# Two PSUM banks for the first pair's keys and queries, and one rotary product from GpSimd to VectorE

## The chip, the cores and the metric

One core of a Trainium2 chip runs the whole kernel. The metric is the device time of one execution in microseconds (us), as the median of several runs. The engines are named as the profile names them: PE is TensorE (PEld its weight loads), DVE is VectorE, ACT is ScalarE, POOL is GpSimd and SP is SyncE, which here only issues DMAs. Each engine works through its own instructions in a fixed order and waits on semaphores for the others.

## What is computed

One encoder layer on 512 tokens of width 1024, in float32: layer norm, one input projection, latent attention with 8 heads beside a convolution branch, an output projection with a residual norm, and a mixture of 16 experts. The part around the change, cut from the reference:

```python
h = layer_norm(x, emb_ln_g, emb_ln_b)
proj = jnp.einsum('bsd,df->bsf', h, w_in[l])
# attention: proj[..., :c1] gives queries, proj[..., c1:c2] keys and values, proj[..., c2:c3] the rotary key
q = jnp.einsum('bsr,rf->bsf', rms_norm(cq, q_norm_g), w_qb).reshape(B, S, H, QK_NOPE_DIM + QK_ROPE_DIM)
kv = jnp.einsum('bsr,rf->bsf', rms_norm(ckv, kv_norm_g), w_kvb).reshape(B, S, H, QK_NOPE_DIM + V_HEAD_DIM)
q = jnp.concatenate([q[..., :QK_NOPE_DIM], rope(q[..., QK_NOPE_DIM:], positions)], axis=-1)
k_pe = jnp.broadcast_to(rope(kr[:, :, None, :], positions), (B, S, H, QK_ROPE_DIM))
k = jnp.concatenate([kv[..., :QK_NOPE_DIM], k_pe], axis=-1)
# softmax(q k^T) v, in blocks of 128 queries
# convolution branch: a * sigmoid(g), depthwise conv of width 31, layer norm, silu
mix = jnp.einsum('bsf,fd->bsd', jnp.concatenate([attn_out, conv_out], axis=-1), w_o[l])
h = layer_norm(DEEPNORM_ALPHA * h + mix, ln1_g[l], ln1_b[l])
h = layer_norm(DEEPNORM_ALPHA * h + expert_choice_moe(h, ...), ln2_g[l], ln2_b[l])
```

`rope` multiplies the rotary part by cosines and adds the part with swapped halves multiplied by sines.

## The kernel before

The work falls into two stages. The first ends near 273.6 us with the routing of tokens to experts. The second runs the 16 experts in turn (L1205 for gate and up, L1291 for down), 2048 KB of weights per DMA, through a ring of tiles that were used by the first stage (`stream`, L128; its DMAs are issued at L135, L145 and L161).

In the first stage nearly every product is made of three matmuls (`mm3`, L260 to L264): operands are split into a high part, copied by ScalarE, and a low part, a subtraction on another engine (`split`, L230 to L232). A projection of the input (`project`, L404) is 24 matmuls into one PSUM bank. A bank is one tile of 128x512 float32, and there are eight: three named `pj`, two `tr`, and one each of `st`, `cn` and `cv` (`bank`, L270).

Around the change the program reads, in this order. `rotary(0)` and `rotary(1)` (L604) make the rotary parts of the queries of four heads each, in bank `cn`: 9 matmuls, then `rope` (L515): ScalarE copies the bank to `raw` (L517), VectorE shuffles it (L519), POOL multiplies `raw` by the cosines (L520), VectorE multiplies the shuffled copy by the sines (L521) and adds the two (L522), and the result is split. `rope` is also used once before, for the rotary key. `glu(3, 4)` (L434) makes the last of four convolution groups: two projections in two `pj` banks, a tanh on ScalarE that reads the second (L439), a product on VectorE that reads the first (L440), four taps on ScalarE and POOL (L448, L449, L451) and 27 on VectorE (L457), marked as filler, which is taken when nothing else is due. Then come copies of the rotary key into the key tiles (L629 on POOL, L631 on ScalarE), `keys(0)` with 6 matmuls and `queries(0)` with 9 (`heads`, L638), each in one bank that two high parts on ScalarE and two low parts on VectorE empty, the V tiles (L659: four times 6 matmuls, each in a `pj` bank, copied out at L663), and the attention itself: `scores` (L737, two `pj` banks a step), `transpose_p` (L754, bank `tr`), `p_v` (L770). Keys and queries of the later pairs use bank `cn`, with the attention running. Behind it stand the first half of the output projection (`output(0, ...)`, L860, with L872), the convolution's norm (L801, L814), whose result feeds the second half, and the routing.

The order of instructions on each engine isn't that of the text. A planner takes the instruction with the earliest place in the program among those it holds ready by a simulated clock, gives out banks in the same pass, and only the stretches marked as ordered keep a written order. The order on the chip is then fixed.

Of the kernel before, what the change touches and what calls it, by code (L numbers as in the profile page):

```python
# [12 lines left out]
OP = mybir.AluOpType  # L13
# [33 lines left out]
def layer_kernel(ctx, tc, x, positions, emb_ln_g, emb_ln_b, w_in, q_norm_g, w_qb, kv_norm_g, w_kvb,  # L47
                 conv_w, conv_b, conv_ln_g, conv_ln_b, w_o, ln1_g, ln1_b, w_router,
                 w_gate, w_up, w_down, ln2_g, ln2_b, rope_rows, out):
    nc = tc.nc  # L50
# [34 lines left out]
    def quarters(t):  # L85
        return [t[:, j * 512:(j + 1) * 512] for j in range(4)]
# [23 lines left out]
    def quarter_tile(q, dt=F32):  # L110
        return slots.tile([128, S], dt, name=f"q{q}")

    def pair_tile(dt=F32R):
        return slots.tile([128, 2, S], dt, name="sq", bufs=2)
# [115 lines left out]
    def split(hi, lo, src, eng):  # L230
        scalar(nc.scalar.activation(hi, src, AF.Identity))  # L231
        pin(eng, eng.tensor_tensor(lo, src, hi.bitcast(F32), op=OP.subtract))  # L232
# [27 lines left out]
    def mm3(p, a, b, start, stop, **kw):  # L260

        tensor(nc.tensor.matmul(p, a[0], b[0], start=start, stop=False, **kw))  # L262
        tensor(nc.tensor.matmul(p, a[0], b[1], start=False, stop=False, **kw))  # L263
        tensor(nc.tensor.matmul(p, a[1], b[0], start=False, stop=stop, **kw))  # L264

    with ExitStack() as pre:
# [3 lines left out]
        def bank(kind="pj"):  # L270
            return ps.tile([128, 512], F32, name=kind, bufs={"pj": 3, "tr": 2, "st": 1, "cn": 1, "cv": 1}[kind])
# [3 lines left out]
        def tmp():  # L275
            n_tmp[0] += 1
            return quarter_tile(n_tmp[0] % 4)
# [34 lines left out]
        def split_win(g):  # L312

            name, c0, n = WIN_GROUPS[g]
            raw = raws.pop(g)
            hi, lo = (slot(i, F32R).rearrange("p (c n) -> p c n", c=8) for i in win_slots[g % 4])
            for j in range(2):
                win[c0 + 128 * j] = (hi, lo, 128 * j)
                for a in range(2):
                    cs, ns = slice(4 * a, 4 * a + 4), slice(128 * j, 128 * j + 128)  # L320
                    if name == "q2" and j:
                        for c in range(4 * a, 4 * a + 4):
                            kb = raw[:, c, None, 128:160].to_broadcast([128, 4, ROPE])
                            h4, l4 = (z[:, c, 128:].rearrange("p (r n) -> p r n", r=4) for z in (hi, lo))
                            nc.scalar.activation(h4, kb, AF.Identity)
                            pin(nc.gpsimd, nc.gpsimd.tensor_tensor(l4, kb, h4.bitcast(F32), op=OP.subtract))
                    else:
                        split(hi[:, cs, ns], lo[:, cs, ns], raw[:, cs, ns], nc.gpsimd)
                    yield
# [28 lines left out]
        def run(*gens):  # L358
            for g in gens:
                for _ in g:  # L360
                    pass
# [31 lines left out]
        for c in range(DC):  # L393
            p = bank("tr")
# [9 lines left out]
        def project(c0, kind="pj"):  # L404
            p = bank(kind)
            hi, lo, j = win[c0]
            for c in range(DC):
                mm3(p, (hi[:, c, j:j + 128], lo[:, c, j:j + 128]), hT[c], c == 0, c == DC - 1)
            return p
# [24 lines left out]
        def glu(j, n_act=0):  # L434

            pa = project(QR + KVR + ROPE + j * 128)
            pg = project(QR + KVR + ROPE + CC + j * 128)
            sg = tmp()
            nc.scalar.activation(sg, pg, AF.Tanh, scale=0.5)  # L439
            nc.vector.scalar_tensor_tensor(hp[j][:, CW // 2:CW // 2 + S], sg, 1.0, pa, op0=OP.add, op1=OP.mult)  # L440
            src = [hp[j][:, k:k + S] for k in range(CW)]
            w = [cw[:, j, k:k + 1] for k in range(CW)]

            part = bank("cv")
            for k in range(n_act):
                if k:
                    pt = tmp()
                    nc.scalar.activation(pt, src[k], AF.Identity, scale=w[k])  # L448
                    nc.gpsimd.tensor_tensor(cva[j], cva[j], pt, op=OP.add)  # L449
                else:  # L450
                    nc.scalar.activation(cva[j], src[k], AF.Identity, scale=w[k], bias=vc("cb", j))  # L451
            with filler():
                for k in range(n_act, CW):
                    if k == 0:
                        nc.vector.tensor_scalar(part, src[k], w[k], vc("cb", j), op0=OP.mult, op1=OP.add)
                    else:
                        nc.vector.scalar_tensor_tensor(part if k < CW - 1 else cva[j], src[k], w[k],  # L457
                                                       cva[j] if k == n_act else part, op0=OP.mult, op1=OP.add)


        sinS, cosT = lat[2:]
# [50 lines left out]

        shuf = [(i + 16) % 32 for i in range(32)]

        def rope(p, dst):  # L515
            raw = tmp()
            nc.scalar.activation(raw, p, AF.Identity)  # L517
            sh = tmp()
            nc.vector.stream_shuffle(sh, raw, shuf)  # L519
            nc.gpsimd.tensor_tensor(raw, raw, cosT, op=OP.mult)  # L520
            nc.vector.tensor_tensor(sh, sh, sinS, op=OP.mult)  # L521
            nc.vector.tensor_tensor(sh, raw, sh, op=OP.add)  # L522
            split(dst[0], dst[1], sh, nc.gpsimd)
# [20 lines left out]
        for j in range(2):  # L544
            p = project(QR + j * 128)
# [4 lines left out]
        pk = project(QR + KVR)  # L550
        add_up(pst, sq)
        kpe = (quarters(s17)[3], quarter_tile(4, F32R))
        rope(pk, kpe)
        run(split_win(5))

        wq_raw = []
# [9 lines left out]
        for j in range(3):  # L566
            p = project(j * 128)
# [33 lines left out]
                split(hi, lo, wkvb[:, c, :].rearrange("p (h f) -> p h f", h=HEADS)[:, :, o:o + 64], nc.gpsimd)  # L601
        qr = {}

        def rotary(g):  # L604
            p = bank("cn")
            for c in range(3):
                w = tuple(wqr[c][:, k * 256 + g * 128:k * 256 + (g + 1) * 128] for k in range(2))
                mm3(p, w, cqn[c], c == 0, c == 2)
            qr[g] = pair_tile()
            rope(p, (qr[g][:, 0], qr[g][:, 1]))  # L610

        rotary(0)
        rotary(1)
        glu(3, 4)


# [28 lines left out]
        def keys(i, kind="cn"):  # L645
            qe, ke, qo, ko = qk[i % 2]
            heads(i, wkn, 2, ckvn, ke, ko, kind)

        def queries(i, kind="cn"):
            qe, ke, qo, ko = qk[i % 2]  # L650
            heads(i, wqn, 3, cqn, qe, qo, kind)
            for n, dst in ((2 * (i % 2), [z[64:96] for z in qe]), (2 * (i % 2) + 1, [z[32:64] for z in qo])):
                for k in range(2):
                    copy_to(k, dst[k], qr[i // 2][32 * n:32 * n + 32, k, :].bitcast(F32), 32 * n)

        keys(0, "pj")
        queries(0, "pj")
        vt = quarters(slot(14))
        for i in range(4):  # L659
            p = bank()  # L660
# [45 lines left out]
        for a in range(2):  # L706
            nc.vector.tensor_tensor(wr2[:, :, a], wr2[:, :, 1], gb[:, a * DC:(a + 1) * DC, None].to_broadcast([128, DC, E]),
                                    op=OP.mult)
# [452 lines left out]
    for e in range(E):  # L1161
# [19 lines left out]
        for k, j in order:  # L1181
            p = pgu[k]
# [76 lines left out]
        for b in range(2):  # L1259
            p = ps.tile([128, 512], F32, name="sg", bufs=2) if b else ps.tile([128, 512], F32, name="tr")  # L1260
# [19 lines left out]
        for c in range(8):  # L1280
# [4 lines left out]
            for a in range(2):  # L1285
                f = 2 * c + a
                b, g, j = f // 8, (f // 4) % 2, f % 4
# [66 lines left out]
```

## Time and profile before

| | us |
|---|---|
| median of 3 runs | 1196.94 (1196.2 to 1197.55) |
| profiled execution | 1194.84 |
| its span, first to last instruction | 1192.4 |
| PE busy | 1119.9 |
| DVE busy | 383.5 |
| ACT busy | 249.6 |
| POOL busy | 200.4 |
| start of the first expert's gather | 273.6 |

Times in the views are counted from the start of the span. Busy time of PE is modelled, since its matmuls are pipelined: back to back they follow one another faster than each one's shown duration. In a timeline a row gives start, duration, engine, line, operation, output and inputs by name, the count of merged instructions, and in brackets the idle time ahead of it and what ended that.

### The profile page before, as it was taken

The numbers are of one execution on the slowest core, as the hardware profiler recorded it, in microseconds if no ns is written. First come the engines' busy times: TensorE is split into PE (matmuls) and PEld (weight loads), VectorE is DVE, ScalarE is ACT, GpSimd is POOL, SyncE is SP. The second block draws the span as 40 slices with busy tenths as digits, with TensorE's granted clock in tenths as the row PEclk, the third lists the DMA queues.
The fourth block names the chain that finished last, engine by engine and source line by source line (L and its number), as shares of the span: only waits on it lengthen the run. The fifth ranks groups of instructions, "written<-read, shape, count | busy, mean of one in ns | idle before, by whom it ended". The sixth has DMA issues, their size and how long they took to land.

```text
span 1192.4 us, 13664 instructions
## 1 busy us (share of the span) xinstructions
PE 1119.9 (94%) x5573; PEld 526.4 (44%) x5573; DVE 383.5 (32%) x901; ACT 249.6 (21%) x461; POOL 200.4 (17%) x234
## 2 busy tenths in 40 slices
PE   5898998999999999999999999989998999899996
PEld 3687775785434343433433343324332423243422
DVE  6899998452110311131012102110311031102241
ACT  4545687321101110100110011001110101012110
POOL 6768577210000600000000000000000000000040
PEclk9999999999999999999999999999999999999999
DMA  6421024777999999999999999999999999999997
GB/s 201 138 73 45 10 72 159 271 272 293 378 426 428 428 428 425 428 429 429 426 426 428 426 427 429 428 426 428 427 428 427 428 429 426 427 428 429 427 426 304
DMA packets 43825, 422.85 MB, mean 355 GB/s; under 512 B 5194, under 2 KB 13203, under 8 KB 18034
## 3 DMA queue, kind: packets, MB, share of 16 engines
q1 hardware_dynamic: 41600, 419.18, 84.8%
q10 hardware_dynamic: 2082, 2.53, 0.6%
q8 instruction: 43, 0.70, 0.2%
q0 software_dynamic: 80, 0.26, 0.1%
q14 instruction: 20, 0.16, 0.0%
HBM read 419.60 MB, written 2.36 MB: 354 GB/s over the span
## 4 chain that ended last, share of the span: by engine, by line
PE 56%; DMA 31%; DVE 9%; ACT 2%; issue 1%; POOL 1%; ACTq 0%; POOLq 0%; SPq 0%; DVEq 0%
PE gu L1205 24%; DMA b<-in_w_up_dram 16%; PE py L1291 13%; DMA b<-in_w_down_dram 9%; PE sg L1048 4%; DVE cv L457 4%; DMA b<-in_w_gate_dram 3%; PE sg L1095 3%; PE pj L262 2%; PE pj L263 2%; PE pj L264 2%; PE st L776 1%; DMA s<-in_w_in_dram 1%; PE tr L1070 1%; ACT s L231 1%
## 5 line engine op out<-in xcount | busy, mean ns | idle before, releaser
L1205 PE MATMUL gu<-b,xg 128*64 128x512 f32 x1920 | 447.1, 600 | 29.2 <-DMA b<-in_w_up_dram 20.2
L1205 PEld LDWEIGHTS gu<-b,xg 128*64 128x64 f32 x1920 | 124.5, 136 | 268.9 <-issue 206.0
L1291 PE MATMUL py<-b,sq 128*64 128x512 f32 x976 | 227.3, 601 | 1.1 <-DMA b<-in_w_down_dram 1.0
L1060 POOL COPY sq<-oh 128x256 f32<-128x256 f32 x16 | 5.9, 400 | 747.1 <-PE sg L1262 747.1
L1291 PEld LDWEIGHTS py<-b,sq 128*64 128x64 f32 x976 | 62.8, 136 | 104.7 <-issue 91.2
L1085 DVE SCALAR_TENSOR_TENSOR q<-py,gates,q 64x512 fp32r<-64x512 f32 x30 | 22.5, 749 | 235.5 <-ACT q L1084 235.5
L262 PE MATMUL pj<-s,s 128*128 128x512 f32 x189 | 76.5, 413 | 9.8 <-ACT q L439 5.3
L1048 PEld LDWEIGHTS sg<-oh,h 128*128 128x128 f32 x512 | 65.3, 197 | 45.5 <-issue 43.8
L1048 PE MATMUL sg<-oh,h 128*128 128x128 f32 x512 | 76.5, 293 | 1.3 <-DVE oh L1039 0.7
L1222 DVE TENSOR_TENSOR sq<-sq,gu 128x512 f32<-128x512 f32 x30 | 20.6, 687 | 175.2 <-PE gu L1205 175.2
L263 PE MATMUL pj<-s,s 128*128 128x512 f32 x189 | 75.7, 401 | 0.0
L1098 DVE TENSOR_TENSOR b<-sg,b 128x512 f32<-128x512 f32 x64 | 43.9, 690 | 85.9 <-PE sg L1095 81.7
L232 POOL TENSOR_TENSOR s<-s,s 128x512 fp32r<-128x512 f32 (+2 forms) x54 | 65.6, 1239 | 16.0 <-ACT s L231 11.0
L1266 ACT ACTIVATE sq<-tr 128x512 f32<-128x512 f32 x16 | 9.6, 597 | 275.6 <-PE tr L1262 275.6
L1049 ACT ACTIVATE xg<-sg,gbp 128x128 f32<-128x128 f32 x64 | 29.2, 457 | 163.0 <-PE sg L1048 163.0
L457 DVE SCALAR_TENSOR_TENSOR cv<-s,q,cv 128x512 f32<-128x512 f32 x83 | 62.2, 750 | 1.7
L264 PE MATMUL pj<-s,s 128*128 128x512 f32 x157 | 61.9, 397 | 0.0
L1227 ACT ACTIVATE sq<-gu 128x512 f32<-128x512 f32 x32 | 18.9, 597 | 189.6 <-PE gu L1205 189.5
L244 DVE SCALAR_TENSOR_TENSOR mask<-tr,aff,ones_b 128x128 bf16<-128x128 f32 x84 | 26.1, 348 | 100.6 <-PE tr L242 100.6
L1095 PE MATMUL sg<-q,q 128*128 128x512 f32 (+1 forms) x128 | 44.9, 448 | 0.3 <-DVE b L1098 0.3
L262 PEld LDWEIGHTS pj<-s,s 128*128 128x128 f32 x189 | 36.4, 194 | 19.3 <-ACT q L439 6.3
L1084 ACT ACTIVATE q<-py,gates 64x512 fp32r<-64x512 f32 x30 | 20.5, 682 | 93.0 <-PE py L1291 72.7
(287 smaller groups left out, 1095.1 us busy)
## 6 DMA issues: line engine op xcount, KB each, us to landing
b<-in_w_gate_dram SPq DMA_DIRECT2D x60, 2048.0 KB, 33.6
b<-in_w_up_dram SPq DMA_DIRECT2D x60, 2048.0 KB, 31.8
b<-in_w_down_dram SPq DMA_DIRECT2D x59, 2048.0 KB, 33.8
s<-in_w_gate_dram SPq DMA_DIRECT2D x8, 1024.0 KB, 6.5
s<-in_w_in_dram SPq DMA_DIRECT2D x12, 512.0 KB, 5.3
s<-in_w_up_dram SPq DMA_DIRECT2D x6, 1024.0 KB, 7.0
s<-in_w_down_dram SPq DMA_DIRECT2D x6, 1024.0 KB, 10.3
s<-in_w_o_dram SPq DMA_DIRECT2D x4, 1024.0 KB, 7.4
```

What stands on the lines that cost most here:

```text
L232: pin(eng, eng.tensor_tensor(lo, src, hi.bitcast(F32), op=OP.subtract))
L244: vector(nc.vector.scalar_tensor_tensor(mask[:, u], here, aff[:, u, e:e + 1], ones_b if u < t else before, op0=OP.is_le, op1=OP.mult, accu ...
L262: tensor(nc.tensor.matmul(p, a[0], b[0], start=start, stop=False, **kw))
L263: tensor(nc.tensor.matmul(p, a[0], b[1], start=False, stop=False, **kw))
L264: tensor(nc.tensor.matmul(p, a[1], b[0], start=False, stop=stop, **kw))
L457: nc.vector.scalar_tensor_tensor(part if k < CW - 1 else cva[j], src[k], w[k], cva[j] if k == n_act else part, op0=OP.mult, op1=OP.add)
L1048: tensor(nc.tensor.matmul(here, rows, oh[:, t, :], start=t == 0, stop=t == TT - 1))
L1049: nc.scalar.activation(xg[:, cc, :], here, AF.Identity, scale=gbp[:, 0, cc:cc + 1], bias=gbp[:, 1, cc:cc + 1])
L1095: tensor(nc.tensor.matmul(pp[h], g[h][rs, ts], parts[h][k][rs, :], start=k == 0, stop=k == 1))
L1098: nc.vector.tensor_tensor(a, pp[h], a, op=OP.add)
L1205: tensor(nc.tensor.matmul(p[b][g * 64:(g + 1) * 64, :], xg[:, c, s * CAP:(s + 1) * CAP], ws[a][2 * b + g], start=c == 0, stop=c == DC - 1))
L1291: tensor(nc.tensor.matmul(py[x * 64:(x + 1) * 64, :], hT2[:, b, j, g * 64:(g + 1) * 64], w[2 * a + hf], start=f == 0 and not last, stop=f ...
```

## The change

`rope` and `rotary` take the engine for the product by the cosines as an argument. The rotary key and the first set of queries pass POOL, as before; the second set passes VectorE. `keys(0)` and `queries(0)` take banks named `tr` where they took `pj`.

```diff
-        def rope(p, dst):
+        def rope(p, dst, eng):
             raw = tmp()
             nc.scalar.activation(raw, p, AF.Identity)
             sh = tmp()
             nc.vector.stream_shuffle(sh, raw, shuf)
-            nc.gpsimd.tensor_tensor(raw, raw, cosT, op=OP.mult)
+            eng.tensor_tensor(raw, raw, cosT, op=OP.mult)
             nc.vector.tensor_tensor(sh, sh, sinS, op=OP.mult)
             nc.vector.tensor_tensor(sh, raw, sh, op=OP.add)
             split(dst[0], dst[1], sh, nc.gpsimd)
...
-        rope(pk, kpe)
+        rope(pk, kpe, nc.gpsimd)
...
-        def rotary(g):
+        def rotary(g, eng):
...
-            rope(p, (qr[g][:, 0], qr[g][:, 1]))
-
-        rotary(0)
-        rotary(1)
+            rope(p, (qr[g][:, 0], qr[g][:, 1]), eng)
+
+        rotary(0, nc.gpsimd)
+
+        rotary(1, nc.vector)
         glu(3, 4)
...
-        keys(0, "pj")
-        queries(0, "pj")
+
+        keys(0, "tr")
+        queries(0, "tr")
```

## Rows read from the trace of the kernel before

**Rows 1.** The page: busy us of each engine, share of the span, instructions.
```profile
PE 1119.9 (94%) x5573; PEld 526.4 (44%) x5573; DVE 383.5 (32%) x901; ACT 249.6 (21%) x461; POOL 200.4 (17%) x234
```

**Rows 2.** Busy time by stretch, in the header's order, with granted clock and DMA.
```profile
core 0: us, PE busy (x) PEld busy (x) DVE busy (x) ACT busy (x) POOL busy (x), PEclk, DMA share, GB/s
100.00:112.40 12.40, 12.40 (x56) 10.06 (x54) 12.19 (x20) 7.47 (x13) 11.71 (x11) 1.00 0.00 0
112.40:128.00 15.60, 9.98 (x38) 7.74 (x38) 15.32 (x23) 10.77 (x19) 14.44 (x12) 0.89 0.11 35
128.00:180.00 52.00, 51.53 (x320) 38.80 (x320) 49.03 (x84) 39.85 (x86) 30.27 (x45) 1.00 0.12 42
180.00:215.00 35.00, 30.97 (x193) 20.75 (x189) 28.49 (x48) 24.77 (x53) 22.54 (x24) 1.00 0.54 183
...
273.60:500.00 226.40, 224.61 (x1137) 92.06 (x1137) 34.62 (x120) 28.53 (x52) 21.34 (x20) 1.00 0.96 403
500.00:1192.00 692.00, 653.14 (x3161) 245.32 (x3157) 131.33 (x377) 71.86 (x126) 19.03 (x25) 1.00 1.00 422
```

**Rows 3.** Timeline of PE, 112 to 128 us: start, duration, instruction, idle before.
```profile
112.16 0.39 PE L264 MATMUL pj<-s,s 128*128 128x512 f32 x1
...
116.08 0.79 PE L262 MATMUL pj<-s,s 128*128 128x512 f32 x1 [3.35 <-ACT q L439]
...
120.82 0.39 PE L264 MATMUL pj<-s,s 128*128 128x512 f32 x1
...
123.81 0.47 PE L262 MATMUL pj<-s,s 128*128 128x512 f32 x1 [2.27 <-DVE s L232]
...
127.99 0.40 PE L262 MATMUL pj<-s 96*128 96x512 f32 x1
```

**Rows 4.** Timeline of ACT, 115 to 123 us.
```profile
115.46 0.57 ACT L439 ACTIVATE q<-pj 128x512 f32<-128x512 f32 x1
...
117.91 0.81 ACT L451 ACTIVATE s<-hp,q 128x512 f32<-128x512 f32 x1 [1.41 <-DVE hp L440]
...
122.30 0.63 ACT L231 ACTIVATE sq<-q 128x512 fp32r<-128x512 f32 x1 [1.73 <-DVE q L522]
```

**Rows 5.** Timeline of DVE, 110 to 123 us.
```profile
110.49 0.73 DVE L519 STREAM_SHUFFLE q<-q 128x512 f32<-128x512 f32 x1
...
111.76 0.82 DVE L521 TENSOR_TENSOR q<-q,s 128x512 f32<-128x512 f32 x1
...
117.20 0.67 DVE L440 SCALAR_TENSOR_TENSOR hp<-q,pj 128x512 f32<-128x512 f32 x1
...
119.06 3.21 DVE L522 TENSOR_TENSOR q<-q,q 128x512 f32<-128x512 f32 x1
...
122.97 0.69 DVE L232 TENSOR_TENSOR s<-pj,s 64x512 fp32r<-64x512 f32 x1
```

**Rows 6.** Timeline of POOL, 112 to 122 us.
```profile
112.10 5.03 POOL L629 TENSOR_TENSOR s<-sq,zero 32x512 fp32r<-32x512 f32 x4
117.20 1.29 POOL L520 TENSOR_TENSOR q<-q,s 128x512 f32<-128x512 f32 x1
118.45 2.03 POOL L629 TENSOR_TENSOR s<-q,zero 64x512 fp32r<-64x512 f32 x2
120.44 1.27 POOL L730 TENSOR_TENSOR h<-h,s 128x512 f32<-128x512 f32 x1
```

**Rows 7.** Line 522 over the span: duration in ns, lowest, median and highest.
```profile
L522 DVE TENSOR_TENSOR q<-q,q x3: 676/687/3215, 74.3 to 119.1; 128x512 f32<-128x512 f32 x3
```

**Rows 8.** Timeline of POOL and DVE, 224 to 233 us.
```profile
224.78 2.67 POOL L232 TENSOR_TENSOR sq<-s,s 128x512 fp32r<-128x512 f32 x2 [0.33 <-ACT s L231]
...
232.42 0.69 DVE L872 SCALAR_TENSOR_TENSOR h<-h,pj 128x512 f32<-128x512 f32 x1 [2.03 <-PE pj L264]
```

**Rows 9.** Groups of instructions, 60 to 215 us: busy us, mean ns, idle before.
```profile
L457 DVE SCALAR_TENSOR_TENSOR cv<-s,q,cv 128x512 f32<-128x512 f32 x76 | 57.0, 750 | 1.6
```

**Rows 10.** What the DMA queue of SP waited for, 60 to 330 us.
```profile
SPq L161 <- PE gu L1205: 25.9, 6, 6.1
```

## The prediction

> **What bounds the kernel now.** I read four views, from coarse to fine. The engine totals come first [rows 1]: TensorE is busy for 94% of the span and nothing else comes near, but that is a mean over stages with different limits. The table by stretches [rows 2] separates them. From 500 us on the DMA engines are full (share 1.00, 422 GB/s) and TensorE does 653 us of work in 692: the experts run at the pace of their weights. From 273.6 to 500 TensorE (224.6 of 226.4) and the DMA (0.96) are both full. So the expert stage has a fixed length, counted from its start: its ring of weight tiles refills only as experts' matmuls free tiles [rows 10], and a microsecond won or lost ahead of 273.6 moves the end by about one microsecond. The change lies ahead of it, so the question is what ends last between 100 and 273.6.
>
> There [rows 2] TensorE is full from 100 to 112.4, has 51.5 us of work in the 52 from 128 to 180, and 31.0 in the 35 from 180 to 215. The one large hole is from 112.4 to 128: 9.98 us of 15.6, at a granted clock of 0.89, so part of it at 1.2 instead of 2.4 GHz. VectorE is nearly full all the while (12.2 of 12.4, 15.3 of 15.6, 49.0 of 52). A large part of that, 57.0 us between 60 and 215 in its largest group alone, is the depthwise convolution (L457), which fills every gap [rows 9]. So I look for what TensorE waits for in the hole, and for what VectorE may still carry.
>
> **The hole, step by step.** TensorE issues its last matmul of the fourth GLU projection at 112.16, apart from one tiny transpose does nothing until 116.08, and is released by ScalarE's tanh (L439) [rows 3]. The 15 matmuls that follow, to 120.82, are 9 of queries(0) and 6 of the first V tile, so keys(0) is already done and queries(0) waits for a `pj` bank: there are three, the projection's two halves hold two and keys(0) the third. The tanh comes at 115.46 with no idle time ahead of it on ScalarE [rows 4]: it stands behind a run of copies. The 15 matmuls then take 4.96 us (116.08 to 121.04, one step after the last one's start); at the pace of the full stretch before, 56 instructions in 12.4 us or 0.22 us each [rows 2], they take 3.3. The second wait, 2.27 us to 123.81, is a V tile waiting for a bank that VectorE's low part (L232, 122.97) frees [rows 3, 5]. That one is late because VectorE stands in L522, the last step of the second rotary set, from 119.06 for 3.21 us. The first score matmul comes at 127.99 [rows 3].
>
> **Part 1, the banks.** keys(0) and queries(0) take the two `tr` banks. Their earlier user, the transposes of the input, is long over, and their next user, the transposes of the probabilities, needs the splits of keys and queries through the scores anyway; this adds no wait. queries(0) then needs no bank of the projection's and follows at 112.4; the first V tile goes to the `pj` bank that keys(0) used to hold. Those 15 matmuls end at 112.4 + 3.3 = 115.7, against 121.04: 5.3 us earlier, of which about 3.7 is the wait and 1.6 the slower matmuls after it. The next V tile takes the bank that the tanh leaves at 116.0 (115.46 + 0.57 [rows 4]), the third the one that L440 leaves at 117.9 [rows 5], the fourth that of the first once it is copied out.
>
> What is late next is ScalarE and VectorE, not TensorE. If only matmuls counted, the scores would start at 112.4 + 33 × 0.22 (queries, four V tiles) + 0.6 for the small transposes = 120.3, which is 7.7 us earlier: one end. The other end is no gain at all, the scores at 128.0: the splits (L231, L232) need ScalarE and VectorE, whose order is fixed in advance and holds the copies ahead of the tanh. In between I count ScalarE: in the hole it idles 15.6 - 10.77 = 4.8 us [rows 2], all of it behind the tanh, of which 1.41 is a wait for L440 and 1.73 a wait for L522 [rows 4], and the rest waits for V tiles and low parts. Without idle time its work from 115.46 to 128.0 is 12.5 - 4.8 = 7.7 us and ends at 123.2; keeping the wait for L440, which VectorE's order sets and the change doesn't touch, 124.6. Some 0.6 of that work (one V tile) needn't come ahead of the scores, which gives about **124.0, a gain of 4.0 us**. I take this because it is nearest to rows that stay.
>
> **Part 2, the product by the cosines.** For the second set, POOL loses one L520 of 1.29 us (at 117.20) [rows 6] and VectorE gains one 128x512 product. POOL's op ran 6 us after its input was shuffled (110.49 [rows 5]), behind 5.03 us of copies [rows 6]; on VectorE it can follow the shuffle at once. No other engine's wait is added: VectorE now waits for ScalarE's copy only, which it did for the shuffle. The first set's product and the key's stay on POOL. The trace shows no such product on VectorE, but L521 and L522 are the same form: L522 took 676, 687 and 3215 ns [rows 7]. So the cost is 0.68 to 3.2 us; I take 0.7. Against it L522 no longer stands at 119.06, and if it then costs 0.69 instead of 3.21, VectorE wins 2.5. Net: 1.8 us less on VectorE, in a stretch where it is full. The two parts meet there: without that stall the low parts and L440's followers come sooner, which is already in the 124.0.
>
> Why 3.21? While L522 stood, POOL ran copies and one L730 from 118.45 to 121.71, and L522 ended 0.6 us after [rows 5, 6]: two SBUF operands on VectorE waited for POOL to come to rest. The Trainium skill (SBUF — State Buffer, section "Who interferes with whom") says that a VectorE instruction with two SBUF inputs contends with a GpSimd instruction that reads SBUF, and that the second to issue blocks fully. This trace agrees (3.21 against 0.68), and it speaks against the change: the new product is such an instruction and comes at 111 to 112, in the middle of POOL's copies. By that rule at its mildest the sum would be as above, and at its worst it is the second rival below.
>
> **Does the gain reach 273.6?** From 128 to 215 TensorE is nearly full, so its start is what counts. The convolution must not fall behind: its last group is split on POOL by 227.5, while the first half of the output projection occupies TensorE until 232.4 [rows 8], and the last group is needed only 9 matmuls (2.0 us) after that. That is a slack of 6.9 us. Attention moved 4.0 us earlier displaces, if half of VectorE's time is filler, about 2.0 us of it, and Part 2 gives back 1.8. So 4.0 fits in 6.9, and 7.7 would not. I keep 4.0.
>
> **The sum.** The profiled execution took 1194.84 us (its span 1192.4 and 2.4 around it), 2.1 less than the median of 1196.94. By it 1194.84 - 4.0 = 1190.8; on the median's scale 1196.94 - 4.0 = 1192.9, which I forecast as **1193.0**.
>
> **Rivals.**
> 1. *The wait only changes its name.* Scores wait for both splits, and ScalarE reaches the tanh no earlier, so they start at 126 or later; or VectorE, nearly full from 100 to 180, returns the gain as a late convolution. For it: ScalarE's copies ahead of the tanh, VectorE at 94 to 98%. Against it: 5 us of ScalarE's time there are waits, two of which hang on the banks and the stall. Gain 0 to 2.4, so 1194.6 to 1197.
> 2. *Slower: VectorE's product is locked out by POOL's copies.* If at 111.3 it stands, as L522 did, until POOL rests at about 117.2, it costs 5.9 us more, with L440 (hence two banks), the low parts and the convolution queued behind it. VectorE would lose 5.9 + 0.7 and win 2.5: 4.1 us later for all that it feeds. TensorE's early queries don't help then, because the scores need the low parts: 128 + 2 to 4, so 1199 to 1201. It decides from a block of about 2.5 us (what the old stall gives back). Against it: L521, at 111.76 and among the same copies, took 0.82 [rows 5].
> 3. *Nothing is done by the banks*, since queries(0) is held by something else than a bank. Against it: the releaser is the tanh, which queries(0) has no data from [rows 3]. I give this 3%, within rival 1.
>
> A further uncertainty belongs to all: instructions are put in order by a planner, so a different bank or engine can also reorder neighbours, by a few microseconds either way. I spread it over the cases.
>
> **How the numbers follow.** The forecast's case (gain 2.4 to 7.7: 1189.2 to 1194.5) has 0.53, rival 1 (with 3) 0.27, rival 2 and unlucky orders 0.20. A measurement of this kernel can tell about 0.2%, 2.4 us, from no change; so faster 0.53, same 0.27, slower 0.20. The range takes the forecast's case from its end, rival 1 whole, and about half of rival 2: 1189.0 to 1199.0. The likeliest case alone is 1189.2 to 1194.5.
>
> **What would show it.** In the changed profile: no wait for L439 in front of queries(0) and a granted clock near 1.00 from 112 to 120; the second set's product a VectorE row of about 0.7 us near 111 to 113, not 3; L522 behind it at 0.69; the first score matmul near 124; POOL without L520 near 117; the first expert's gather about 4 us earlier. I would be wrong if the scores start near 124 but the output projection doesn't (the convolution then ended last), or if VectorE shows a new row of 3 us or more among POOL's copies.

## The result, and the profile after

The changed kernel takes 1213.81 us (median of 4 runs, 1210.78 to 1215.51) where the kernel before takes 1196.57 (4 runs): a ratio of 1.0147, 95% interval 1.0129 to 1.0164, so **17.2 us slower**. Its profiled execution took 1210.78 with a span of 1209.0, 16.6 more than before's span. The first expert's gather starts at 290.02 instead of 273.64, 16.4 later: practically all of it is lost ahead of the expert stage, as [rows 2, 10] let one expect. In the program after, L630 is before's L629, and lines from L663 on carry numbers higher by 2 (L693 is L695, L707 is L709, L747 is L749, L869 is L871).

The banks did in place what was forecast. Timeline of PE in the changed kernel (start, duration, instruction, idle ahead of it and what ended that):

```profile
121.96 0.50 PE L262 MATMUL pj<-s 96*128 96x512 f32 x1
...
126.75 0.77 PE L263 MATMUL pj<-s 128*128 128x512 f32 x1 [3.05 <-DVE s L232]
...
130.37 3.59 PE L715 MATMUL cn<-q,q 128*128 128x32 f32 x16 [0.99 <-DVE q L712]
...
135.19 1.06 PE L763 MATMUL tr<-ident,s 128*128 128x128 f32 x4
```

The first score comes at 121.96, 6.0 us ahead of before's 127.99 [rows 3]. But the second group of scores waits 3.05 us for a low part from VectorE, the 16 small matmuls of the router's constants (L715) stand next in PE's order and wait for VectorE too, and the first transpose of the probabilities is issued at 135.19, where before's was at 132.55. Six microseconds ahead became 2.6 behind in thirteen. TensorE's clock fell with the waits: from 127 to 135 us the granted clock is 0.50, its level of 1.2 GHz, where before's is 1.00, and the 16 router matmuls take 3.59 us instead of 1.87.

VectorE is why TensorE waits there. Its timeline in the changed kernel, 110 to 129 us, and POOL's under it:

```profile
110.65 1.55 DVE L520 TENSOR_TENSOR q<-q,s 128x512 f32<-128x512 f32 x1
112.12 1.52 DVE L521 TENSOR_TENSOR q<-q,s 128x512 f32<-128x512 f32 x1
...
115.02 1.52 DVE L522 TENSOR_TENSOR q<-q,q 128x512 f32<-128x512 f32 x1
...
121.12 2.21 DVE L695 COPY gb<-q 128x32 f32<-128x32 f32 x1
...
123.90 1.98 DVE L709 TENSOR_TENSOR q<-q,gb 128x128 f32<-128x128 f32 x1
```

```profile
111.71 5.73 POOL L630 TENSOR_TENSOR s<-sq,zero 32x512 fp32r<-32x512 f32 x4
117.52 2.03 POOL L630 TENSOR_TENSOR s<-q,zero 64x512 fp32r<-64x512 f32 x2
119.51 1.29 POOL L732 TENSOR_TENSOR h<-h,s 128x512 f32<-128x512 f32 x1
120.77 1.27 POOL L232 TENSOR_TENSOR sq<-q,sq 128x512 fp32r<-128x512 f32 x1
```

POOL works without a gap from 111.7 to 125.7. The new product takes 1.55 us instead of 0.7, L521 1.52 (before 0.82 [rows 5]), L522 1.52 (before 3.21 [rows 5]). Then two small instructions that nobody had counted appear as long ones: the copy L695 of 128x32 takes 2.21 us and the first product L709 of 128x128 takes 1.98. These are their rows in the kernel before, where they came at 114.7 and 115.5, beside POOL's 32x512 copies [rows 6]:

```profile
114.74 0.23 DVE L693 COPY gb<-q 128x32 f32<-128x32 f32 x1
...
115.54 0.62 DVE L707 TENSOR_TENSOR q<-q,gb 128x128 f32<-128x128 f32 x1
...
116.75 0.53 DVE L707 TENSOR_TENSOR q<-q,gb 128x128 f32<-128x128 f32 x1
...
192.91 0.74 DVE L457 SCALAR_TENSOR_TENSOR s<-hp,q,cv 128x512 f32<-128x512 f32 x1
```

So VectorE's account against before reads: +1.55 (L520) +0.70 (L521) -1.69 (L522) +1.98 (L695) +1.12 (the two L709, 1.98 and 0.29, against 0.62 and 0.53) = **+3.7 us**, where the prediction had -1.8. The last row above is before's last convolution tap, at 192.91. After's is the first row below, 11.2 us later. The second row is the first step of the convolution's norm on VectorE, which waits 5.27 us for TensorE's sums:

```profile
204.14 0.73 DVE L457 SCALAR_TENSOR_TENSOR s<-hp,q,cv 128x512 f32<-128x512 f32 x1
...
219.52 2.48 DVE L806 SCALAR_TENSOR_TENSOR s<-cn,s 128x512 f32<-128x512 f32 x4 [5.27 <-PE cn L493]
```

The table by stretches of the changed kernel (columns as in [rows 2]), and under it that of before for stretches of the same bounds, shows where TensorE lost time:

```profile
128.00:150.00 22.00, 21.01 (x99) 16.01 (x98) 17.50 (x33) 13.85 (x29) 7.17 (x13) 0.76 0.00 1
215.00:240.00 25.00, 20.87 (x103) 16.04 (x102) 11.41 (x17) 5.54 (x8) 3.80 (x4) 0.93 0.40 157
```

```profile
128.00:150.00 22.00, 21.94 (x130) 16.66 (x129) 20.48 (x36) 15.70 (x34) 7.38 (x14) 1.00 0.00 1
215.00:240.00 25.00, 24.25 (x114) 19.91 (x115) 11.60 (x18) 7.53 (x11) 7.64 (x7) 1.00 0.75 282
```

From 128 to 150 TensorE looks full, but it gets through 99 instructions instead of 130 at a granted clock of 0.76, after the waits shown above. VectorE idles 4.5 us there instead of 1.5: its order is fixed with score maxima ahead of taps, so when scores are late the taps stand still too. From 215 to 240 TensorE has 4.1 us without work instead of 0.8, and a lower clock again. The chain that ended last tells what that was (start, length, what; the changed kernel, with rows left out at the dots):

```profile
219.05 0.44 PE cn L493
...
220.13 1.88 DVE s L806 x3
...
227.28 0.54 PE cn L493
...
236.02 0.23 PE cn L493
...
242.44 0.61 DVE s L821
...
245.19 1.28 POOL sq L232
246.52 0.79 PE pj L264
```

The convolution's norm needs two channel sums (L493), each of two matmuls. The second matmul of the first sum had its operands by 212.4 (POOL's split at 211.11, 1.29 long) but stands behind other matmuls, attention's last products among them, in PE's fixed order until 218.98. The second sum starts at 227.28; its second matmul had its operands by 228.6 (POOL's split at 227.30, 1.30 long) and stands behind matmuls of the output projection's first half until 235.86. The norm's factor is ready at 239.45 (POOL's L502 at 238.43, 1.02 long), and the four small transposes that spread it (L509) stand behind the rest of that half until 241.55. These three waits in the queue make about 16 us. Only then can the convolution be normed, passed through SiLU (L821, L823), split on POOL and fed to the second half of the projection, whose first result VectorE reads at 251.52 instead of 235.14. In before the chain from 219 to 236 us is matmuls of the output projection; of the convolution's norm only L502 and L509 stand on it, from 217.03 to 218.75.

So two delays add up. Attention ends later: its last product with V on TensorE (L778) ends at 218.84 us against 213.83 in before, 5.0 later. And the second half follows later behind it: 32.7 us against 21.3, 11.4 longer, because the convolution's norm stands where it does in TensorE's order. Together these are the 16.4 us.

### The profile page after: what moved, and what is told of

Same layout as the page of the kernel before. It is cut to its first block, busy times and chain, and to the rows that moved or that the text cites. A ratio compares the mean times of both kernels' runs of the same rounds, so it can differ in the third digit from the quotient of the medians.

```text
span 1209.0 us, 13664 instructions
## 1 busy us (share of the span) xinstructions
PE 1130.9 (94%) x5573; PEld 532.2 (44%) x5573; DVE 386.9 (32%) x902; ACT 250.4 (21%) x461; POOL 198.1 (16%) x233
## 4 chain that ended last, share of the span: by engine, by line
PE 66%; DMA 25%; DVE 5%; ACT 2%; issue 1%; POOL 1%; ACTq 0%; POOLq 0%; SPq 0%; DVEq 0%
PE gu L1207 25%; DMA b<-in_w_up_dram 15%; PE py L1293 15%; DMA b<-in_w_down_dram 8%; PE sg L1050 6%; PE pj L262 3%; PE pj L264 3%; PE pj L263 3%; PE sg L1097 2%; PE st L778 1%; DVE cv L457 1%; PE tr L763 1%; DMA s<-in_w_in_dram 1%; PE tr L1072 1%; ACT s L231 1%
## 5 line engine op out<-in xcount | busy, mean ns | idle before, releaser
L262 PE MATMUL pj<-s,s 128*128 128x512 f32 x184 | 75.9, 421 | 9.7 <-ACT s L231 6.8
L263 PE MATMUL pj<-s,s 128*128 128x512 f32 x184 | 74.7, 406 | 0.0
L232 POOL TENSOR_TENSOR s<-s,s 128x512 fp32r<-128x512 f32 (+2 forms) x54 | 64.1, 1208 | 16.4 <-ACT s L231 11.6
L457 DVE SCALAR_TENSOR_TENSOR cv<-s,q,cv 128x512 f32<-128x512 f32 x83 | 62.3, 751 | 1.7
L264 PE MATMUL pj<-s,s 128*128 128x512 f32 x152 | 60.2, 400 | 0.0
L262 PEld LDWEIGHTS pj<-s,s 128*128 128x128 f32 x184 | 36.3, 199 | 18.5 <-ACT s L231 7.4
```

## The experiments

All kernels compute everything. Times in the table are starts in us, from each kernel's profile: the first score (L262 on 96 partitions), the first transpose of probabilities (L763; L761 in before), the last tap (L457), VectorE's first read of the output projection's second half, and the gather; attention's end is the end of its last product with V on TensorE (L778; L776 in before). In the two kernels with sums sooner these lines carry numbers higher by 7 again. The ratio is to the kernel before on the same chip.

| kernel | median | ratio [95%] | first score | first transpose | last tap | attention's end | second half | gather |
|---|---|---|---|---|---|---|---|---|
| before | 1196.57 | 1 | 127.99 | 132.55 | 192.91 | 213.83 | 235.14 | 273.64 |
| after | 1213.81 | 1.0147 [1.0129, 1.0164] | 121.96 | 135.19 | 204.14 | 218.84 | 251.52 | 290.02 |
| banks alone | 1203.22 | 1.0057 [1.0040, 1.0074] | 120.19 | 138.88 | 199.17 | 218.84 | 240.15 | 278.48 |
| product alone | 1204.88 | 1.0068 [1.0051, 1.0085] | 130.85 | 135.42 | 197.64 | 216.44 | 244.63 | 283.27 |
| after, sums sooner | 1209.59 | 1.0106 [1.0089, 1.0123] | 121.60 | 134.86 | 202.56 | 217.71 | 249.67 | 289.03 |
| before, sums sooner | 1196.38 | 0.9993 [0.998, 1.0007] | 127.87 | 132.42 | 195.22 | 215.69 | 237.02 | 276.64 |
| after, product from PSUM | 1210.90 | 1.0131 [1.0098, 1.0163] | 120.86 | 134.97 | 203.28 | 218.21 | 250.58 | 290.03 |
| after, constants on POOL | 1201.26 | 1.0038 [1.0020, 1.0055] | 122.71 | 132.44 | 192.12 | 221.17 | 242.69 | 281.19 |
| banks, constants on POOL | 1198.40 | 1.0021 [1.0008, 1.0035] | 120.64 | 129.75 | 188.92 | 216.74 | 238.07 | 276.78 |
| banks, constants and sum on POOL | 1204.07 | 1.0064 [1.0040, 1.0089] | 120.88 | 128.60 | 183.50 | 218.83 | 241.17 | 279.50 |
| before, constants on POOL | 1199.69 | 1.0009 [0.9993, 1.0025] | 130.91 | 135.50 | 199.17 | 220.05 | 241.36 | 280.04 |
| product, constants on POOL | 1194.91 | 0.9972 [0.9960, 0.9983] | 125.31 | 129.87 | 193.21 | 213.37 | 234.69 | 273.19 |
| banks, constants on POOL, maxima | 1212.76 | 1.0124 [1.0102, 1.0146] | 120.25 | 135.71 | 199.55 | 232.31 | 253.64 | 291.99 |
| after, constants on POOL, maxima | 1208.99 | 1.0089 [1.0068, 1.0111] | 121.53 | 133.49 | 204.18 | 227.53 | 248.83 | 288.32 |

A profile is one execution and the median many, so a shift of the gather and a difference of medians can differ, mostly by 2 to 4 us and by 5 in before with its constants on POOL. Differences in us below are of the medians, where no start or end is named; by the ratios they come out the same within 2 us, and verdicts go by the ratios.

The last columns sort the kernels. In ten of the fourteen the second half follows attention's end by 21.3 to 22.3 us. In four, after, product alone, sums sooner in after, and product from PSUM, it takes 28.2 to 32.7, and in these four alone L509 stands in TensorE's order behind the first half of the output projection.

### One part at a time

The banks alone (second rotary set back on POOL):

```diff
-        rotary(1, nc.vector)
+        rotary(1, nc.gpsimd)
```

> Only the banks are changed; the second set's product by the cosines stays on POOL. Theory A (VectorE's product is shut out by POOL's copies, and VectorE's lost time makes the convolution late): without the product the convolution's last tap is back near 193 us and the time is 1190 to 1198. Theory B (the banks themselves: scores start sooner, the max reductions then stand ahead of the convolution's taps on VectorE and wait for TensorE): the time stays at 1207 to 1214. Theory C (neither alone; the planner's new order of the convolution's norm on TensorE): between 1198 and 1207.

The product alone (keys and queries back in `pj`):

```diff
-        keys(0, "tr")
-        queries(0, "tr")
+        keys(0, "pj")
+        queries(0, "pj")
```

> Only the product by the cosines of the second set goes to VectorE; keys and queries stay in the projection's banks. Theory A: 1205 to 1214, the three two-input instructions of the second set at 1.5 us each. Theory B: 1195 to 1199, since 0.7 to 2 us on VectorE are hidden or given back. Theory C: 1198 to 1207.

Each is slower by itself, by 6.6 and 8.3 us; together 14.9 of the 17.2. So neither part is a gain that the other spoils. Both times lie in the range of theory C, and for the product TensorE's rows below fit it. Theory A's sign for the banks, the last tap back near 193, did not come (199.17). For the product alone its sign, three rows of about 1.5 us, came (1.54, 1.52, 1.42), but the largest loss is elsewhere. Two rows of VectorE with the banks alone, two of VectorE with the product alone, and POOL's rows of the run with the product alone:

```profile
118.02 3.41 DVE L522 TENSOR_TENSOR q<-q,q 128x512 f32<-128x512 f32 x1
...
122.01 4.25 DVE L695 COPY gb<-q 128x32 f32<-128x32 f32 x1
```

```profile
116.82 0.36 DVE L695 COPY gb<-q 128x32 f32<-128x32 f32 x1
...
118.35 4.73 DVE L709 TENSOR_TENSOR q<-q,gb 128x128 f32<-128x128 f32 x1
```

```profile
117.21 2.03 POOL L630 TENSOR_TENSOR s<-q,zero 64x512 fp32r<-64x512 f32 x2
119.21 1.28 POOL L732 TENSOR_TENSOR h<-h,s 128x512 f32<-128x512 f32 x1
120.45 1.25 POOL L232 TENSOR_TENSOR sq<-q,sq 128x512 fp32r<-128x512 f32 x1
121.67 1.25 POOL L449 TENSOR_TENSOR s<-s,q 128x512 f32<-128x512 f32 x1
```

In both, a tiny instruction of the router's constants stands for over 4 us. With the product alone the copy L695 still came at 116.8, beside the 32x512 copies, and took 0.36; the product L709 came 1.5 us later, beside 64x512 and 128x512 work, and took 4.73. So the price hangs, as these rows suggest, on where in POOL's run an instruction lands, and each part pushed one of these instructions further into the run. The product did it by its own length. The banks did it by filling the hole on TensorE: the constants begin with the one tiny transpose in that hole (L345), which stood at 112.48 in before and stands behind queries(0) and a V tile at 115.38 with the banks alone and at 115.86 in after.

The table says what became of it. With the banks alone attention ends 5.0 us later and the second half follows as before. With the product alone attention ends 2.6 later, and 6.9 are lost behind it. POOL's last step of the convolution's norm and the transposes that it feeds, with the product alone and then in before:

```profile
223.68 1.02 POOL L502 TENSOR_TENSOR rs<-rs,half_n 128x4 f32<-128x4 f32 x1
...
234.61 0.60 PE L509 MATMUL cn<-ident,rs 128*128 128x128 f32 x4
```

```profile
217.03 1.02 POOL L502 TENSOR_TENSOR rs<-rs,half_n 128x4 f32<-128x4 f32 x1
...
218.10 0.65 PE L509 MATMUL cn<-ident,rs 128*128 128x128 f32 x4 [0.40 <-POOL rs L502]
```

In before TensorE waits for the factor; with the product alone the factor, ready at 224.70, waits 9.9 us for its turn on TensorE. Without that wait it would be 6.6 us later than in before, with attention 2.6 later: 4.0 us, which fit into the prediction's slack of 6.9, so by this estimate the order on TensorE is the whole of the 6.9 us lost there. The planner made that order; why a product on another engine led it there no run here tells.

### The convolution's sums earlier in PE's order

A lower place in the planner's order for the two functions that make the sums, in after and, as a control, in before:

```diff
+    def sooner(by):
+        saved = tc.cur_priority
+        tc.cur_priority = saved - by
+        yield
+        tc.cur_priority = saved + (tc.cur_priority - saved + by)
...
-        pm = conv_mean()
+        with sooner(400):
+            pm = conv_mean()
...
-        pvv = conv_norm(pm)
+        with sooner(400):
+            pvv = conv_norm(pm)
```

> The changed kernel, with the convolution's mean and norm given an earlier place in the planner's list, by 400 places. On TensorE the second matmul of the sum of squares, which stood 35 rows behind the first, follows it directly; nothing else of the work changes. Theory C (that matmul, held in TensorE's queue behind half of the output projection, holds the second half): the first matmul of the second half comes 6 to 8 us sooner and the time is 1203 to 1207. Theories A and B (the convolution's taps are already late by 11 us on VectorE): at most 3 us are won, 1209 to 1214.

> The kernel before with the same earlier place for the convolution's mean and norm. There the two matmuls of each sum already stand close together on TensorE. All theories: within 2 us of the kernel before, 1194 to 1199; more than that would mean that the earlier place itself moves other work.

It gives back 4.2 of the 17.2 us in after and nothing in before; the profile of the first shows less, 1.9 us at the second half and 1.0 at the gather. The time is in the range of theories A and B, but the run does not decide against the queue, because the edit moved the sums and not the transposes behind them:

```profile
226.55 1.03 POOL L509 TENSOR_TENSOR rs<-rs,half_n 128x4 f32<-128x4 f32 x1
...
239.93 0.60 PE L516 MATMUL cn<-ident,rs 128*128 128x128 f32 x4
```

The factor is ready at 227.58 instead of 239.45, and then waits 12.3 us in TensorE's queue behind the first half of the projection (L516 here is after's L509). What after would take with these transposes in their old place was not tried.

### The same product with one operand in PSUM

```diff
-            eng.tensor_tensor(raw, raw, cosT, op=OP.mult)
+            eng.tensor_tensor(raw, p if eng is nc.vector else raw, cosT, op=OP.mult)
```

> The changed kernel, but VectorE's product by the cosines reads the rotary set from its PSUM bank instead of from ScalarE's copy in SBUF: one SBUF operand in place of two, all orders as in the changed kernel. Lock theory (an instruction of VectorE with two SBUF operands waits for POOL's): this row falls from 1.55 us to about 0.7, the two behind it stay at 1.5, and the time falls by 0.5 to 2 us, 1211 to 1213. If the 1.5 us have another cause (the copy's own end, the bank), the row stays at 1.5 and the time at 1214.

VectorE reads the rotary bank instead of its copy; nothing else changes. Timeline of VectorE:

```profile
110.81 0.70 DVE L520 TENSOR_TENSOR q<-cn,s 128x512 f32<-128x512 f32 x1
...
119.82 3.29 DVE L695 COPY gb<-q 128x32 f32<-128x32 f32 x1
```

The product takes 0.70 instead of 1.55, beside the same POOL copies (1.54 to 1.57 in the five other runs that have it on VectorE): the extra time belongs to the second SBUF operand. The Trainium skill (SBUF — State Buffer, section "Who interferes with whom") says so of VectorE instructions with two SBUF inputs beside GpSimd's reads, and exempts those with at most one outside certain modes; this run agrees. Of the two steps behind it, L522 stays at 1.52 as expected; L521, which the edit doesn't touch, fell to 0.95. But the kernel wins 2 or 3 us, which the intervals don't tell from nothing: the copy L695, now at 119.8 instead of 121.1, takes 3.29 instead of 2.21. Of the 1.4 us that the two rows saved, 1.1 are paid to a later instruction that meets POOL's run.

### The router's constants off VectorE

Three small instructions, the copy L695 and the two products L709, go to POOL, where they take 0.20 and 0.39 us each:

```diff
-        nc.vector.tensor_copy(gb, vcol[:, 33:65])
+        nc.gpsimd.tensor_copy(gb, vcol[:, 33:65])
...
-            nc.vector.tensor_tensor(wr2[:, :, a], wr2[:, :, 1], gb[:, a * DC:(a + 1) * DC, None].to_broadcast([128, DC, E]),
+            nc.gpsimd.tensor_tensor(wr2[:, :, a], wr2[:, :, 1], gb[:, a * DC:(a + 1) * DC, None].to_broadcast([128, DC, E]),
```

In after:

> The changed kernel, but the copy of the norms' columns (0.2 us of work) and the two products of the router's weights (0.28 each) are done by POOL itself. In the changed kernel they took 2.21 and 1.98 us on VectorE. Lock theory: VectorE wins 3.7 us at 121 to 126, the low parts of queries(0), the scores' maxima and the convolution's last tap come that much sooner, and with them the sums of the convolution's norm: 1200 to 1208. If the time hangs on the planner's order of the norm's matmuls or on the clock alone: 1210 to 1214.

With the banks alone:

> Banks only, with the same three small instructions on POOL. There the copy took 4.25 us on VectorE and the low parts stood behind it. Lock theory: the first transposes of the probabilities come at 130 to 134 instead of 138.9, near or ahead of the kernel before (132.55), and the time is 1193 to 1198 against 1203. If the banks cost by themselves (scores too early for their maxima): 1201 to 1205.

In before, as a control:

> The kernel before with the three small router instructions on POOL, as a control: there they took 0.23, 0.62 and 0.53 us on VectorE, with 0.7 us of that lost to waiting. Lock theory: the move by itself is worth no more than 0.7 us on VectorE, 1195 to 1199; only where they are locked out for 4 us does it pay. If the move is a gain of its own (another order of the planner, POOL cheaper): 1185 to 1193.

With the product alone:

> Product only, with the three small instructions on POOL. There one of the router's products took 4.73 us on VectorE, ahead of keys(0)'s low part. Lock theory: the first score comes at 126 to 128 instead of 130.85 and the time is 1196 to 1200 against 1204.9. If the product costs by itself on VectorE: 1202 to 1205.

Out of after this takes 12.5 of the 17.2 us (1213.81 to 1201.26), out of the banks alone 4.8 of 6.6, out of the product alone 10.0, more than its whole loss of 8.3. In before, where those instructions cost 0.2 to 0.6, it wins nothing; its one profile even has the gather 6.4 us later. In after with this edit VectorE's account is +1.56 +0.70 -1.69 for the rotary steps and -1.38 for what left, -0.8 in all, and the last tap comes at 192.12, 0.8 ahead of before's. That the two agree is in part chance: from 108 us to there VectorE idles 2.2 us longer, and four row maxima fewer stand ahead of the tap. The product with its constants on POOL beats both kernels, by 0.28% (0.17 to 0.40%) against before, although its rotary steps still take 1.55, 1.52 and 1.42.

So the constants decide, but the edit does two things at once. It takes them out of POOL's way on VectorE, and the planner's order on TensorE changes with it: L509 stands at 222.19 in after with this edit and at 217.65 in the product alone with it, close behind attention's end as in before, and the second half again follows by 21.5 and 21.3 us. That is worth 11.2 and 6.9 us, where these two profiles win 8.8 and 10.1 in all at the gather. The rest shows at attention's end, which comes 3.1 us sooner with the product alone and 2.1 with the banks alone, but 2.3 later in after. No run moves the constants and keeps TensorE's order, so the shares of the lock and of the order are not shown apart.

After with this edit remains slower by 0.38%. Its first transpose comes when before's does, but attention ends 7.3 us later: its router matmuls (L715) now wait 1.83 us for POOL's L709, take 3.62 us, and the clock from 128 to 150 us is 0.79. I didn't separate these.

### Are earlier scores worth anything?

The banks, with the constants on POOL and all rotary sums (L522) there beside the products, so that of the rotary steps VectorE keeps the shuffle and the sines (the edit against after, beside that of the constants):

```diff
-            nc.vector.tensor_tensor(sh, raw, sh, op=OP.add)
+            eng.tensor_tensor(sh, raw, sh, op=OP.add)
...
-        rotary(1, nc.vector)
+        rotary(1, nc.gpsimd)
```

> As the last one, and the sum that ends each rotary set (the 3.4 us row) is done by POOL too, where it cannot be locked out by POOL. Lock theory: another 2 to 3 us less on VectorE ahead of 125 us, 1191 to 1196, faster than the kernel before. Against it: POOL then ends its run 1.3 us later for each of three sets, and if POOL bounds there, 1197 to 1202.

The last tap comes at 183.50, 9.4 us ahead of before, the first score 7.1 ahead, and the kernel is 0.64% slower all the same, beyond both expected ranges. Attention ends 5.0 us later than in before. PE's timeline:

```profile
127.15 0.79 PE L262 MATMUL pj<-s 128*128 128x512 f32 x1 [3.93 <-ACT s L752]
...
128.60 1.05 PE L763 MATMUL tr<-ident,s 128*128 128x128 f32 x4
131.10 0.79 PE L262 MATMUL pj<-s 96*128 96x512 f32 x1 [1.45 <-ACT q L752]
```

Three groups of scores fill the three `pj` banks, and the fourth waits for an exponential (L752), which waits for the negated maximum, a 128x1 product on POOL (L750). The first maximum was ready at 122.6; that product ran at 126.02, behind POOL's 1.25 us instructions. After the wait a matmul takes 0.79 us instead of 0.39; the granted clock from 127 to 135 us is 0.50 here too. So I tried that product on VectorE, with the constants on POOL, with the banks alone and in after:

```diff
-                nc.gpsimd.tensor_tensor(m, m, rq[:, t:t + 1], op=OP.mult)
+                nc.vector.tensor_tensor(m, m, rq[:, t:t + 1], op=OP.mult)
```

> Banks only, router instructions on POOL, and the small product of the row maxima with the norm's factor (128x1, 0.19 us) on VectorE instead of POOL. In the run without this last edit TensorE waited 1.8 us for an exponential whose bias stood in POOL's queue between instructions of 1.3 us. Theory that POOL's run up to 131 us is what early scores wait for: the first matmuls with the probabilities come at 134 to 138 instead of 139.55, and the time is 1188 to 1195, faster than the kernel before. If the early scores wait for ScalarE or VectorE: 1196 to 1200.

> The changed kernel with both of these edits: router instructions on POOL, the maxima's small product on VectorE. Theory that POOL's run bounds the early scores: 1190 to 1198 against 1201.3 without the maxima's edit. If VectorE, with three locked-out rotary instructions of 1.5 us, bounds: 1200 to 1203.

Both are slower than without it, by 12.3 and 6.1 us after their ratios, far above both expected ranges. VectorE and POOL, in the first of them:

```profile
127.22 6.09 DVE L750 TENSOR_TENSOR mx<-mx,rq 128x1 f32<-128x1 f32 x1
...
137.21 0.15 DVE L750 TENSOR_TENSOR mx<-mx,rq 128x1 f32<-128x1 f32 x1
```

```profile
126.45 1.25 POOL L449 TENSOR_TENSOR s<-s,q 128x512 f32<-128x512 f32 x1
...
128.03 2.47 POOL L732 TENSOR_TENSOR h<-h,s 128x512 f32<-128x512 f32 x2
...
132.04 1.25 POOL L732 TENSOR_TENSOR h<-h,s 128x512 f32<-128x512 f32 x1
```

One value per partition, two SBUF operands, 6.09 us, ended when POOL's run without a pause ended (133.29); ten microseconds later the same instruction takes 0.15. It is the plainest view of the lock, but it leaves the question open: what scores at 121 would be worth with POOL free in time for their maxima wasn't tried.

## Why the prediction was wrong, step by step

The forecast was 1193.0, with a range of 1189.0 to 1199.0; the time lies 14.8 us above its end.

**Right:** the wait for the tanh (L439) ahead of queries(0) is gone, and TensorE's granted clock from 112 to 120 us is 1.00 (0.79 before); POOL has no L520 near 117; the first score came at 121.96, between the bounds 120.3 and 128.0, and earlier than the 124.0 taken; what is lost ahead of 273.6 moved the end by as much (16.4 and 16.6 us; 4.8 and 5.0 with the banks alone, 9.6 and 9.8 with the product alone).

**The 3.21 us were misread.** The prediction let POOL come to rest at 121.71, while L522 stood. POOL's next row in before begins right there:

```profile
121.69 1.71 POOL L449 TENSOR_TENSOR s<-s,q 128x512 f32<-128x512 f32 x1
```

POOL ran on without a pause to 127.13. L522, behind POOL's copies and L730 till then, ended 0.6 us into that row, which takes 1.71 us where the next of its line takes 1.28. Nor does POOL rest at 117.2, where the second rival let the block end: L520 follows there. (The matmul at 112.16, given to the GLU projection, is the last of keys(0); nothing hangs on it.)

**The term of the product was mis-sized.** It cost 1.55, not 0.7. It lies within the stated bounds, but the value was taken from L521's 0.82, the shortest of that line's three rows in before (the other two 1.33 and 1.37), which a look at the line over the whole span shows:

```profile
L521 DVE TENSOR_TENSOR q<-q,s x3: 825/1329/1368, 72.4 to 111.8; 128x512 f32<-128x512 f32 x3
```

That short row was luck: with the banks alone, where POOL still makes the product, L521 takes 1.55, so its +0.70 in after isn't the product's doing. L522 did come ahead of its old stall, but at 1.52, not 0.69: 1.7 us won, not 2.5.

**The step that failed is "Net: 1.8 us less on VectorE".** It counted the rotary set alone. With the rest of VectorE's queue in place the account is +3.7, because L695 and L709, which the prediction doesn't name, moved from POOL's 32x512 copies into its 128x512 run, behind the tiny transpose that it did see in the hole. The second rival had the mechanism, but put it on the product, priced it at 1199 to 1201, and let it end at 117.2; in after POOL doesn't rest before 125.7, and what stands in its way is whatever two-operand or copy instruction comes next. Moving the constants away returns 12.5 us, so the loss hangs on them, though a large part of it comes back by TensorE's order (above). Reading one operand from PSUM moved most of the block to a later instruction: the product's own lock is the small part.

**"From 128 to 215 TensorE is nearly full, so its start is what counts" failed.** The start came 6.0 us earlier, was lost by the first transpose, and attention ended 5.0 us later. Full at a given pace isn't full ahead of it: scores begun early wait for low parts, maxima and exponentials. With the last tap at 183.50 and the first score at 120.88 the kernel still was no faster than before.

**"Attention moved 4.0 us earlier displaces ... 2.0 us" failed by size.** The last tap came 11.2 us late. Counted on VectorE from 108 us to there, 3.7 are the rows above, 5.6 more idle time (9.2 against 3.6), mostly ahead of row maxima that wait for scores, and 3.6 other work that now stands ahead of the tap (two row maxima, a low part of 128x512, a copy of transposed probabilities), less 1.6 for two taps done before 108.

**The slack of 6.9 was no safeguard, because the order on TensorE moved.** With the banks alone the last tap is 6.3 us late and nothing is lost behind attention's end; with the product alone it is 4.7 late and 6.9 are lost there. What sets them apart is where L509 stands. That the planner's order can shift neighbours stood in the prediction as "a few microseconds either way", spread over the cases; in after it is the largest item, 11.4 of the 16.4 us, and it went one way.

**What stays open:** why the planner's order on TensorE changes with the product and changes back with the constants, and how much the lock alone would cost in a fixed order; the 4.7 us that after still loses with its constants on POOL; and the 2.3 us by which both parts together exceed the sum of each.

## What to carry to other kernels

When work is moved to an engine that stood, in the trace, while another one worked, make the account over its whole queue for as long as the other one runs without a gap: every later copy or two-operand instruction is moved against that run, and the smallest may pay most. When a planner fixes the order, compare the order of every engine, not only of the one that was edited: here the costliest change was the late place of a few matmuls on TensorE, over 100 us behind the edit. Price a moved operation from all the rows of its form and from what ran beside each, not from the nearest short one. An earlier start is worth only what the next three consumers can take, so follow it as far as the first result that leaves the stage, and take the end of each branch (here attention's end and the convolution's) as a row of its own.

## What the runs showed of the hardware

A VectorE instruction with two SBUF operands, or a copy from SBUF to SBUF, can stand behind several POOL instructions in a row, not one: 4.25, 4.73 and 6.09 us, while no POOL instruction there takes over 1.71. The Trainium skill (SBUF — State Buffer, section "Who interferes with whom") says that whoever issues first has the shared pair "for the whole instruction" and the other blocks; its wording gives one instruction's length, and the measurement decides: here the wait lasted three and more. The price doesn't go by size (128x1 took 6.09, 128x32 4.25) but by what POOL does and by the moment: beside 32x512 copies a 128x128 product took 0.62, beside 64x512 and 128x512 work 4.73, and the second such product of that run, six microseconds later, took only 0.28; it started 0.09 us behind a 128x512 product of POOL that took 1.50. Why those differ no run here tells.
